# The front of a hybrid block rewritten in another order: angles, row statistics, squares and low products

## The chip, the cores and the metric

The kernel runs on one core of a Trainium2 chip. The metric is the device time of one execution in microseconds (us); the profile's own times are in us too, unless marked ns. TensorE is called PE here, its weight loads PEld, VectorE DVE, ScalarE ACT, GpSimd POOL, and SyncE, which issues most of the transfers, SP. L171 is line 171 of the kernel.

## The reference

The block is one layer of a decoder with a final norm: 1024 positions of width 1024. The input is normalised, modulated by a vector that comes from a condition `c`, and multiplied by one wide matrix whose columns feed attention with a window, a gated recurrent branch, and gates.

```python
mod = c @ w_ada[l] + b_ada[l]
shift, scale, gate = jnp.split(mod, 3, axis=-1)
h = rmsnorm(x, norm_g[l]) * (1.0 + scale[:, None, :]) + shift[:, None, :]
proj = h @ w_in[l]
q, k, v, g_attn, xr, g_rnn, m_attn, m_rnn = jnp.split(proj, SPLIT_POINTS, axis=-1)
...
merged = (jax.nn.sigmoid(m_attn) * (y_attn @ w_attn_proj[l])
          + jax.nn.sigmoid(m_rnn) * (y_rnn @ w_rnn_proj[l]))
x = x + gate[:, None, :] * (merged @ w_out[l])
return rmsnorm(x, final_g)
```

`q` and `k` are turned by angles that come from the positions (`partial_rope`). Here only the way to `h`, the first columns of `proj` and the angles matter.

## The kernel before, in words

The order of instructions is written by hand: each engine runs what the program lists for it, in that order, and waits for others by semaphores. The change touches the **front**, from the start of the program to the first products of V.

**Layout.** `h` is kept transposed: 128 input channels on the partitions, the 1024 positions along the free axis, so there are eight channel blocks, `kc` = 0 to 7, called channels below. Every block exists in two halves of 512 positions (`hf` = 0, 1). To multiply with nearly f32 precision, each operand is split in a rounded high part and the remaining low part: `hh` and `hl` for `h`, `wh` and `wl` for the weights. A product is three matmuls of 512 columns: `wh` by `hh` and `wl` by `hh` (terms "h"), and `wh` by `hl` (terms "l"). `hha`, `hhb`, `hla`, `hlb` in the profile are the halves for the channels 0 to 3, `hh` and `hl` both halves for 4 to 7.

**What the front computes.** Four column blocks of `proj` (`starts`), each with two accumulators of 512 positions in PSUM (`pmain` twice, and the banks `bk`), over the eight channels: 4 x 8 x 2 x 3 = 192 matmuls.

**What feeds them.** For channel `kc`:
- `modulate(kc, a)` (L241, DVE) multiplies a block of `w_ada` (`wada`, from `w_ss` in DRAM) with `c` spread over all partitions (`c_bc`) and sums it: a = 0 gives the shift, a = 1 the scale, and after it `gsc` (L245).
- `norm(kc)` (L371, DVE) multiplies the transposed input `xT` with `r_bc`, the root of each position's mean square, spread over the partitions. For channel 0 it reads the bank directly, one half at a time (L368).
- `affine(kc)` (L378, ACT) applies scale and shift in place; `high` (L374) or a cast (L478, ACT) makes `hh`; `low(kc)` (L383, DVE) makes `hl` by subtraction.

**The row statistics.** `x` also comes in eight tiles of 128 positions (`xt`). `square(i)` (L254, ACT) sums the squares of one. When four are done, `mean` (L352, DVE), `root_of` (L357, ACT) and the reciprocal in `spread` (L361, DVE) follow, and four transposes on PE (L363) spread the result over the partitions of a bank. Each half of the positions has its own such step.

**Weights.** `cast_w(i, h)` (L102 or L104, ACT) and `rest_w(i, h)` (L108 or L110, DVE) split half `h` (four channels) of the weights of block `i`. V's weights are split by the same two lines.

**Angles.** `angles()` reduces position times frequency to a turn in 29 small steps on DVE (128 x 64 mostly); the calls of `some(n)` take the next n of its pieces. `table()` takes the sine on ACT (L342) and writes a table to DRAM through POOL's queue.

**Fillers.** Four f32 matmuls of `ident` with `xt` (L421) and one with `r_bc` (L430) write a bank that nobody reads.

**Transfers.** All input loads of the front go through SP's queue in the order written. `wada` and `xt` share seven buffers, the halves of weights (`r`) six; a load into a buffer in use waits on SP, and the ones behind it wait too.

Of the kernel before, what the change touches and what calls it, by code (L numbers as in the profile page):

```python
# [12 lines left out]
F32 = mybir.dt.float32  # L13
# [9 lines left out]
P = 128  # L23
S = 1024
D = 1024
# [13 lines left out]
PAD_S = 544  # L39
# [13 lines left out]
def tile_hybrid_block(ctx, tc, x, x_t, pk, rows, posr, posi, c_row, w_ss, w_gate, w_main, w_v,  # L53
# [4 lines left out]
    def dma(dst, src, eng=nc.sync):  # L58
        dst, src = (a.bitcast(F32) if a.dtype == F32R else a for a in (dst, src))
        return eng.dma_start(dst, src)  # L60
# [126 lines left out]
    with ExitStack() as st:  # L187
# [10 lines left out]
        root = sp.tile([P, 1], F32, name="root")  # L198
        rr = sp.tile([P, 8], F32, name="rr")
# [7 lines left out]

        def load_ss(kc):
            for a in range(2):
                wa_t = sp.tile([P, D + 1], F32, tag="wada", name="wada", bufs=7)  # L210
                dma(wa_t[:], w_ss[a * D + kc * P:a * D + (kc + 1) * P, :])
                wada[kc, a] = wa_t
# [4 lines left out]
        def load_xt(kc):  # L217
            dma(xT[kc][:], x_t[kc * P:(kc + 1) * P, :])
# [6 lines left out]
        load_ss(0)  # L225
        for i in range(4):
            load_x0(i)
        load_xt(0)
        load_wh(0, 0)
# [5 lines left out]
        V.memset(c_bc[:, D:], 1.0)  # L235
        for hf in range(2):
            T.matmul(bk[2 + hf], one[0:1, :], c_row_t[:, SL[hf]], start=True, stop=True)

# [13 lines left out]
        def square(i):  # L252
            junk = sp.tile([P, D], BF16, tag="junk", name="junk")
            A.activation(junk[:], xt[i], AF.Square, accum_out=rr[:, i:i + 1])  # L254

# [94 lines left out]
        def mean(hf):  # L350
            r1 = rr[:, 4 * hf:4 * hf + 4]
            V.tensor_scalar(out=r1, in0=r1, scalar1=1.0 / D, scalar2=EPS, op0=ALU.mult,  # L352
                            op1=ALU.add)

        def root_of(hf):
            r1 = rr[:, 4 * hf:4 * hf + 4]
            A.activation(r1, r1, AF.Sqrt)  # L357
# [47 lines left out]
        some(7)  # L405
        V.tensor_copy(c_bc[:, SL[0]], bk[2])
        some(2)
        V.tensor_copy(c_bc[:, SL[1]], bk[3])
        for a in range(2):
            modulate(0, a)  # L410
        square(0)
        load_x0(5)
        load_x0(6)
        square(1)
        load_x0(7)
        for i in range(1, 4):
            load_wh(i, 0)
        square(2)
# [3 lines left out]
        load_ss(1)  # L422
        load_xt(1)
        mean(0)
        root_of(0)
        some(2)
        spread(0)
        some(2)
        A.copy(r_bc[:, SL[0]], bk[0])
# [4 lines left out]
        load_ss(2)  # L434
        load_xt(2)
        for i in range(2):
            load_wh(i, 1)
        rest_w(0, 0)
        high(0, 0)
# [12 lines left out]
        cast_w(2, 0)  # L452
        high(0, 1)
        affine(0, SL[1])
        rest_w(2, 0)
        A.copy(r_bc[:, SL[1]], bk[1])
        cast_w(3, 0)
        low(0, (1,))
        for a in range(2):
            modulate(1, a)  # L460
            if not a:
                rest_w(3, 0)
        for hf in range(2):
            for i in range(4):
                w, ps = starts[i]
                for ww, xx_ in ((w[0][0], hh), (w[0][1], hh), (w[0][0], hl)):
                    T.matmul(ps[hf], ww[:, 0:P], xx_[0][hf], start=(ww is w[0][0] and xx_ is hh),
                             stop=False)
        load_ss(3)
        load_xt(3)  # L470
# [3 lines left out]
        for kc in range(1, KC):  # L474
            norm(kc)
            affine(kc)
            for hf in range(2):
                A.copy(hh[kc][hf], xT[kc][:, SL[hf]])  # L478
# [10 lines left out]
            if kc + 3 < KC:  # L489
                load_ss(kc + 3)  # L490
                load_xt(kc + 3)
            if kc == 3:
                rv = [load_half(w_v[i // 2][:, SL[i % 2]]) for i in range(4)]
            if kc < 3:
                for terms in ("h", "l"):
                    for w, ps in starts:
                        mm_k(ps, w, kc, terms=terms)
            else:
                for i in (2, 3, 0, 1):
                    w, ps = starts[i]  # L500
# [1325 lines left out]
```

## Time and profile before

| | us |
|---|---|
| Three runs | 933.85, 934.57, 935.89 (median 934.57) |
| The profiled execution's own time | 935.91 |
| Its span in the trace | 934.2 |
| PE busy in the span | 909.0 |
| DVE busy | 680.8 |
| ACT busy | 533.8 |
| First product of the front | 24.39 |
| First product of V, behind the front | 76.85 |

The span is the time from the first to the last instruction of the trace; what lies around it is in the execution's own time. In rows of the timeline the first column is the start in us, the second the duration, then engine, line, operation, what it writes and reads, and the shape; in brackets stands how long the engine was idle just before, and what ended that. Matmuls overlap: of two in a row the second starts before the first has ended, so the distance of their starts is their price. The granted clock is the share of its full clock that PE was given.

### The profile page before, as it was taken

Reading aid. Unit: us, or ns where it says so; the run is one execution under the profiler, and the core shown is the slowest. Engines: PE = TensorE matmul, PEld = TensorE weight load, DVE = VectorE, ACT = ScalarE, POOL = GpSimd, SP = SyncE. Lnnn points to the kernel's source line nnn. Section 1 sums busy time; section 2 is a strip of 40 time slices with the busy share of each in tenths; the row PEclk is TensorE's granted clock in tenths of the full one; section 3 lists DMA queues with packets and bytes.
Section 4 is the critical chain, followed back from the end, with each engine's and each line's share of the span. In section 5 each row is a group of like instructions: output and inputs, shape, how many; then the busy total and the mean of one; then the engine's idle time right before and its main releaser. Section 6 shows DMA issues by size and latency. Waiting matters only on the chain.

```text
span 934.2 us, 12299 instructions
## 1 busy us (share of the span) xinstructions
PE 909.0 (97%) x4227; PEld 749.4 (80%) x4227; DVE 680.8 (73%) x1041; ACT 533.8 (57%) x1028; POOL 86.6 (9%) x146
## 2 busy tenths in 40 slices
PE   5999999999999999999999999999999999999997
PEld 1679888887888888888887888788888888888886
DVE  5895879887768973987688575799999737657422
ACT  5552566554557755875687785788888622213211
POOL 0120000000000000000000001354454300000000
PEclk9899999999999999999999999999999999999998
DMA  9942457864323351354245258997656186536311
GB/s 353 414 180 92 145 193 252 282 235 145 113 80 124 135 192 34 122 161 169 72 142 191 73 185 270 328 330 218 225 178 191 57 313 223 163 121 239 135 72 63
DMA packets 82147, 168.39 MB, mean 180 GB/s; under 512 B 12755, under 2 KB 29139, under 8 KB 82086
## 3 DMA queue, kind: packets, MB, share of 16 engines
q1 hardware_dynamic: 78596, 159.47, 50.0%
q0 software_dynamic: 2192, 6.00, 1.9%
q10 hardware_dynamic: 1298, 2.15, 0.6%
q8 instruction: 33, 0.54, 0.2%
q14 instruction: 28, 0.23, 0.1%
HBM read 118.20 MB, written 49.78 MB: 180 GB/s over the span
## 4 chain that ended last, share of the span: by engine, by line
PE 78%; DVE 9%; DMA 8%; ACT 2%; issue 2%; POOL 0%; SPq 0%; ACTq 0%; DVEq 0%
PE bk L648 43%; PE rp L171 8%; PE pgate L942 5%; PE rp L1689 4%; PE bk L171 4%; PE pmain L1689 4%; PE s_ps L1192 2%; PE pv L1264 2%; DMA smr<-smr_d 2%; PE pmain L171 1%; DMA wo<-w_out 1%; DMA tt<-tr_d 1%; PE pt L1230 1%; DVE wl L108 1%; DMA r<-w_ap 1%
## 5 line engine op out<-in xcount | busy, mean ns | idle before, releaser
L648 PE MATMUL bk<-nh,wl 128*128 128x512 f32 x352 | 137.3, 390 | 0.4 <-DVE wl L108 0.4
L648 PE MATMUL bk<-nh,wh 128*128 128x512 f32 x352 | 137.1, 389 | 0.0
L648 PE MATMUL bk<-nl,wh 128*128 128x512 f32 x352 | 137.0, 389 | 0.0
L108 DVE TENSOR_TENSOR wl<-r,wh 128x512 fp32r<-128x512 f32 x109 | 78.9, 729 | 23.3 <-ACT wh L102 23.3
L102 ACT CAST wh<-r 128x512 fp32r<-128x512 f32 x109 | 66.9, 618 | 42.3 <-PE bk L1437 13.2
L648 PEld LDWEIGHTS bk<-nh,wl 128*128 128x128 f32 x352 | 66.1, 188 | 15.0 <-DVE wl L108 1.4
L648 PEld LDWEIGHTS bk<-nh,wh 128*128 128x128 f32 x352 | 66.1, 188 | 13.7
L648 PEld LDWEIGHTS bk<-nl,wh 128*128 128x128 f32 x352 | 66.1, 188 | 13.6
L648 PE MATMUL bk<-hh,wh 128*128 128x512 f32 x176 | 68.6, 390 | 0.0
L648 PE MATMUL bk<-hh,wl 128*128 128x512 f32 x176 | 68.5, 389 | 0.0
L648 PE MATMUL bk<-hl,wh 128*128 128x512 f32 x176 | 68.5, 389 | 0.0
L108 DVE TENSOR_TENSOR wl<-ws,wh 128x512 fp32r<-128x512 f32 x76 | 51.5, 683 | 0.5 <-ACT wh L102 0.5
L1216 ACT ACTIVATE p<-p,small 128x129 f32<-128x129 f32 x128 | 50.1, 401 | 0.0
L102 ACT CAST wh<-ws 128x512 fp32r<-128x512 f32 x76 | 45.8, 614 | 3.3 <-DMA hla<-yl_d 1.6
L60 POOL DMA_DIRECT2D yh_d<-yh x1 | 0.6, 555 | 494.6 <-ACT yh L1009 494.6
L1706 ACT ACTIVATE o<-xo 128x1024 f32<-128x1024 f32 (+2 forms) x10 | 8.9, 889 | 53.2 <-DVE xo L1705 53.2
L648 PEld LDWEIGHTS bk<-hh,wh 128*128 128x128 f32 x176 | 33.0, 188 | 7.7 <-ACT wh L102 0.9
L648 PEld LDWEIGHTS bk<-hl,wh 128*128 128x128 f32 x176 | 33.0, 188 | 6.9
L648 PEld LDWEIGHTS bk<-hh,wl 128*128 128x128 f32 x176 | 33.0, 188 | 6.8
L1192 PE MATMUL s_ps<-ks,qs 128*128 128x256 f32 (+1 forms) x256 | 37.6, 289 | 0.1
L751 ACT ACTIVATE c<-bk 128x512 f32<-128x512 f32 x29 | 17.3, 597 | 30.3 <-PE bk L648 30.2
L648 PE MATMUL bk<-hha,wl 128*128 128x512 f32 x88 | 34.4, 390 | 0.1
(383 smaller groups left out, 2287.0 us busy)
## 6 DMA issues: line engine op xcount, KB each, us to landing
r<-w_main SPq DMA_DIRECT2D x100, 256.0 KB, 4.2
wada<-w_ss SPq DMA_DIRECT2D x16, 512.5 KB, 8.2
qs<-q_d SPq DMA_DIRECT2D x16, 512.0 KB, 5.9
ks<-k_d SPq DMA_DIRECT2D x24, 192.0 KB, 3.9
xT<-x_t SPq DMA_DIRECT2D x8, 512.0 KB, 8.8
q_d<-rhi SPq DMA_DIRECT2D x16, 256.0 KB, 4.1
q_d<-rlo SPq DMA_DIRECT2D x16, 256.0 KB, 3.7
sma_d<-c SPq DMA_DIRECT2D x16, 256.0 KB, 2.5
```

The costliest lines, as they stand in the source:

```text
L102: A.copy(dst[0][:], src)
L108: V.tensor_tensor(out=dst[1][:], in0=src, in1=f32(dst[0][:]), op=ALU.subtract)
L171: mm = T.matmul(ps[hf], ww, xx[kc][hf], start=(kc == 0 and ww is w_h and xx is xh), stop=(kc == KC - 1 and xx is xl))
L648: W["pe"] = T.matmul(ps, ww[:, c], b[kc][xx_], start=(first and kc == 0 and i == 0), stop=(kc == 3 and i == 2), skip_group_check=not first)
L751: A.activation(t["t"], s(), AF.Tanh, scale=0.5)
L942: W["pe"] = T.matmul(ps[:, SL[hf]], ww[:, c0:c0 + P], xx_[:, SL[hf]], start=(ic == 0 and i == 0), stop=(ic == 1 and i == 2))
L1192: W["pe"] = T.matmul(o, qs[:, j, qc], ks[:, b, k0 + (0 if n else P):k0 + 256], start=(b == 0), stop=(b == 1))
L1216: A.activation(px[:, j, :], px[:, j, :], AF.Exp, bias=sm[:, 0, j:j + 1], accum_out=sm[:, 1, j:j + 1])
L1230: W["pe"] = T.transpose(pt[:, j, :], px[:, j, 0:P], ident[:])
L1264: W["pe"] = T.matmul(pv[:], b, m[:].rearrange("p j q -> p (j q)"), start=(i == 0), stop=(i == len(prods) - 1))
L1689: T.matmul(ps[:, sl], lhs[k][th][:, ts_], w[:, sl], start=(k == 0 and w is h_ and lhs is mh), stop=(k == KC - 1 and lhs is ml))
L1706: A.activation(o[:, sl], xo[:, sl], AF.Square, accum_out=fs[:, i:i + 1])
```

## The change

It rewrites the front; the mathematics stays. In the order of the program:

- **Angles** (`some`): 22 of the steps stand ahead of modulate(0, 0), the other seven behind it. Before they were dealt out over the first 23 us.
- `c_bc` is copied out of the bank by ACT instead of DVE. The two `wada` of channel 0 are loaded apart, the second behind `xT` of channel 0.
- **Squares**: 5 and 7 go to DVE (`square_v`), the others stay on ACT. `mean` goes, and its factor and epsilon become scale and bias of the root.
- **Fillers** go.
- `spread(1)` follows `root_of(1)` at once, so that its transposes stand on PE behind the first two products; both copies of `r_bc` follow it on ACT.
- **norm** is called one channel ahead: norm(kc + 1) stands in the pass of `kc`, ahead of modulate(kc + 1). For channel 1 `high` makes `hh` straight from `xT`, before `affine`.
- **Low products one channel behind**: PE takes the "h" terms of `kc`, then the "l" terms of `kc` - 1.
- `xT` and `wada` are loaded a channel sooner, `xT` first; the second halves of the weights later; V's weights last. V's rests all stand behind the loop. `table()` moves from channel 1 to 2.

```diff
-        load_ss(0)
+        load_a(0, 0)
         for i in range(4):
             load_x0(i)
         load_xt(0)
+        load_a(0, 1)
         load_wh(0, 0)
         load_x0(4)
...
+            A.copy(c_bc[:, SL[hf]], bk[2 + hf])
...
+        def square_v(i):
+            jk = sp.tile([P, D + 1], BF16, tag="junk2", name="jk")
+            V.scalar_tensor_tensor(out=jk[:, :D], in0=xt[i], scalar=1.0, in1=xt[i],
+                                   op0=ALU.mult, op1=ALU.mult, accum_out=rr[:, i:i + 1])
...
-            A.activation(r1, r1, AF.Sqrt)
+            A.activation(r1, r1, AF.Sqrt, scale=1.0 / D, bias=eps[:])
...
+        some(16)
         square(0)
-        load_x0(5)
-        load_x0(6)
+        modulate(0, 0)
+        for i in (5, 6, 7):
+            load_x0(i)
+        for i in range(1, 4):
+            load_wh(i, 0)
         square(1)
-        load_x0(7)
-        for i in range(1, 4):
-            load_wh(i, 0)
         square(2)
+        some(99)
+        load_xt(1)
+        load_ss(1)
         square(3)
-        for i in range(4):
-            T.matmul(bk[1], ident[:], xt[i][:, :HALF], start=True, stop=True)
...
+        modulate(0, 1)
+        load_xt(2)
+        load_ss(2)
         root_of(0)
-        some(2)
         spread(0)
-        some(2)
-        A.copy(r_bc[:, SL[0]], bk[0])
-        T.matmul(bk[1], ident[:], r_bc[:, SL[0]], start=True, stop=True)
         cast_w(0, 0)
         norm(0, 0)
+        high(0, 0)
+        rest_w(0, 0)
+        terms_of(0, 0, (0,), "h")
         square(4)
+        square_v(5)
         affine(0, SL[0])
-        square(5)
         low(0, (0,))
-        some(99)
         square(6)
-        square(7)
-        mean(1)
+        square_v(7)
         root_of(1)
+        spread(1)
         cast_w(1, 0)
-        spread(1)
+        A.copy(r_bc[:, SL[0]], bk[0])
         rest_w(1, 0)
+        A.copy(r_bc[:, SL[1]], bk[1])
         norm(0, 1)
...
         for kc in range(1, KC):
-            norm(kc)
-            affine(kc)
-            for hf in range(2):
-                A.copy(hh[kc][hf], xT[kc][:, SL[hf]])
             if kc == 1:
+                for hf in range(2):
+                    high(kc, hf)
+                affine(kc)
+            else:
+                affine(kc)
+                for hf in range(2):
+                    A.copy(hh[kc][hf], xT[kc][:, SL[hf]])
+            if kc == 2:
                 table()
             if kc + 1 < KC:
+                norm(kc + 1)
                 for a in range(2):
                     modulate(kc + 1, a)
...
+            if kc == 1:
+                for hf in range(2):
+                    terms_of(kc, hf, range(4), "h")
+            elif kc < KC - 1:
+                for w, ps in starts:
+                    mm_k(ps, w, kc, terms="h")
+                for w, ps in starts:
+                    mm_k(ps, w, kc - 1, terms="l")
             else:
-                for i in (2, 3, 0, 1):
-                    w, ps = starts[i]
-                    mm_k(ps, w, kc)
+                last = [starts[i] for i in (2, 3, 0, 1)]
+                for w, ps in last:
+                    mm_k(ps, w, kc, terms="h")
+                for w, ps in last:
+                    for k in (kc - 1, kc):
+                        mm_k(ps, w, k, terms="l")
             if kc in (5, 6, 7):
                 for i in ((0,), (1,), (2, 3))[kc - 5]:
-                    wv.append(split(slot(), rv[i]))
+                    wv.append(slot())
+                    cast(wv[i], rv[i])
+        for i in range(4):
+            rest(wv[i], rv[i])
```

Three places of the new order matter below. The first is DVE's queue between the first scale and the first low part of channel 0, before (`rr` are the sums of squares, `sb`, `tt` and the like steps of the angles, `wl` a rest of weights):

```order
L241 SCALAR_TENSOR_TENSOR jk_276,mods_216<-wada_226,c_bc_212 128x1025
L245 SCALAR_TENSOR_TENSOR gsc_217<-mods_216,pk_t_75 128x1
L352 TENSOR_SCALAR rr_219<-rr_219 128x4
L270 TENSOR_SCALAR ra_309<-sa_269 128x64
L276 TENSOR_TENSOR fa_311<-sa_269,ra_309 128x64
L361 RECIPROCAL rr_219<-rr_219 128x4
L299 TENSOR_SCALAR sb_318<-t2_256 128x64
L302 SCALAR_TENSOR_TENSOR sb_318<-t1_260,sb_318 128x64
L302 SCALAR_TENSOR_TENSOR sb_318<-t0_264,sb_318 128x64
L315 TENSOR_TENSOR tt_322<-fa_311,sb_318 128x64
L368 TENSOR_TENSOR xT_190<-xT_190,bk0_68 128x512
L108 TENSOR_TENSOR wl_327<-r_237,wh_326 128x512
```

The same place of the changed kernel, down to norm(0, 1) and one rest behind it:

```order
L248 SCALAR_TENSOR_TENSOR jk_328,mods_216<-wada_236,c_bc_212 128x1025
L252 SCALAR_TENSOR_TENSOR gsc_217<-mods_216,pk_t_75 128x1
L368 RECIPROCAL rr_220<-rr_220 128x4
L375 TENSOR_TENSOR xT_190<-xT_190,bk0_68 128x512
L108 TENSOR_TENSOR wl_343<-r_238,wh_342 128x512
L265 SCALAR_TENSOR_TENSOR jk_352,rr_220<-xt_298 128x1024
L390 TENSOR_TENSOR hla0_160<-xT_190,hha0_158 128x512
L265 SCALAR_TENSOR_TENSOR jk_358,rr_220<-xt_301 128x1024
L368 RECIPROCAL rr_220<-rr_220 128x4
L108 TENSOR_TENSOR wl_372<-r_303,wh_371 128x512
L375 TENSOR_TENSOR xT_190<-xT_190,bk1_69 128x512
L110 SCALAR_TENSOR_TENSOR wl_379<-r_305,wh_378 128x512
```

The angles and the mean are gone from here, two squares (L265) stand between, and modulate(0, 1) with its scale is the row right ahead of the first reciprocal.

The second place is DVE's queue in the pass of channel 3, before (`xT3_193` is channel 3, `xT_194` channel 4):

```order
L371 TENSOR_TENSOR xT3_193<-xT3_193,r_bc_188 128x1024
L241 SCALAR_TENSOR_TENSOR jk_523,mods_216<-wada_446,c_bc_212 128x1025
L241 SCALAR_TENSOR_TENSOR jk_525,mods_216<-wada_448,c_bc_212 128x1025
L245 SCALAR_TENSOR_TENSOR gsc_217<-mods_216,pk_t_75 128x1
L110 SCALAR_TENSOR_TENSOR wl02_208<-r_425,wh02_207 128x512
L110 SCALAR_TENSOR_TENSOR wl03_210<-r_427,wh03_209 128x512
L383 TENSOR_TENSOR hla3_172<-xT3_193,hha3_170 128x512
L383 TENSOR_TENSOR hlb3_173<-xT3_193,hhb3_171 128x512
```

And in the changed kernel:

```order
L378 TENSOR_TENSOR xT_194<-xT_194,r_bc_188 128x1024
L248 SCALAR_TENSOR_TENSOR jk_516,mods_216<-wada_422,c_bc_212 128x1025
L248 SCALAR_TENSOR_TENSOR jk_518,mods_216<-wada_424,c_bc_212 128x1025
L252 SCALAR_TENSOR_TENSOR gsc_217<-mods_216,pk_t_75 128x1
L110 SCALAR_TENSOR_TENSOR wl02_208<-r_426,wh02_207 128x512
L110 SCALAR_TENSOR_TENSOR wl03_210<-r_428,wh03_209 128x512
L390 TENSOR_TENSOR hla3_172<-xT3_193,hha3_170 128x512
L390 TENSOR_TENSOR hlb3_173<-xT3_193,hhb3_171 128x512
```

Only the first row differs: it is norm of channel 4 where it was norm of channel 3.

The third place is PE's queue at the first products of channel 3 with the banks 2 and 3, before:

```order
L171 MATMUL bk2_70<-hha3_170,wh_379 128x512
L171 MATMUL bk3_71<-hhb3_171,wh_379 128x512
L171 MATMUL bk2_70<-hha3_170,wl_380 128x512
L171 MATMUL bk3_71<-hhb3_171,wl_380 128x512
L171 MATMUL bk2_70<-hla3_172,wh_379 128x512
L171 MATMUL bk3_71<-hlb3_173,wh_379 128x512
```

In the changed kernel, from the last "h" terms of channel 3 on:

```order
L171 MATMUL bk0_68<-hha3_170,wl_385 128x512
L171 MATMUL bk1_69<-hhb3_171,wl_385 128x512
L171 MATMUL pmain_254<-hla2_168,wh_342 128x512
L171 MATMUL pmain_254<-hlb2_169,wh_342 128x512
L171 MATMUL pmain_255<-hla2_168,wh_371 128x512
L171 MATMUL pmain_255<-hlb2_169,wh_371 128x512
```

Before, `hla3` is read by the fifth product of the channel; now all sixteen "h" terms of channel 3 and the eight "l" terms of channel 2 run first, and `hla3` is read after the "h" terms of channel 4.

More of the change, by code (lines that the diff above doesn't have):

```diff
@@ L453, in tile_hybrid_block @@
         high(0, 1)
+        rest_w(2, 0)
         affine(0, SL[1])
-        rest_w(2, 0)
-        A.copy(r_bc[:, SL[1]], bk[1])
         cast_w(3, 0)
+        norm(1)
+        modulate(1, 0)
+        rest_w(3, 0)
         low(0, (1,))
[L459 to L462, printed above, removed]
-        for hf in range(2):
-            for i in range(4):
-                w, ps = starts[i]
[L466 to L470, printed above, removed]
+        modulate(1, 1)
+        terms_of(0, 0, (0,), "l")
+        for i in (1, 2, 3):
+            for terms in "hl":
+                terms_of(0, 0, (i,), terms)
+        terms_of(0, 1, range(4), "h")
+        terms_of(0, 1, range(4), "l")
+        for i in range(2):
+            load_wh(i, 1)
+        load_xt(4)
+        load_ss(4)
         for i in (2, 3):
```

56 lines of the change are left out of this document (23 added, 33 removed).

## The prediction

> **What bounds the kernel now.** I read the busy shares first, then the busy time by stretch, then TensorE (PE) and VectorE (DVE) in order of time.
>
> ```profile
> PE 909.0 (97%) x4227; PEld 749.4 (80%) x4227; DVE 680.8 (73%) x1041; ACT 533.8 (57%) x1028; POOL 86.6 (9%) x146
> ...
> 24.30:76.90 52.60, 49.04 (x196) 38.21 (x195) 44.34 (x73) 28.60 (x42) 8.41 (x13) 0.93 0.68 264
> 76.90:130.00 53.10, 53.00 (x324) 47.50 (x323) 38.56 (x54) 26.37 (x41) 0.00 (x0) 1.00 0.44 153
> 130.00:934.20 804.20, 794.33 (x3691) 658.58 (x3689) 585.11 (x870) 464.37 (x920) 77.45 (x127) 1.00 0.51 171
> ```
>
> In the stretches the columns are length, busy time of PE, its weight loads, DVE, ScalarE (ACT) and GpSimd, then granted clock, DMA share and GB/s. After 76.9 us PE is busy almost all the time, so the program is bound by TensorE's own products there. The change touches only what lies ahead. There 192 products of 512 columns must run, and they take from 24.39 to 76.85.
>
> ```profile
> 24.39 0.78 PE L467 MATMUL pmain<-hha,wh 128*128 128x512 f32 x1
> ...
> 48.69 0.75 PE L171 MATMUL bk<-hla,wh 128*128 128x512 f32 x1 [1.50 <-DVE hla L383]
> ...
> 52.33 0.39 PE L171 MATMUL pmain<-hha,wh 128*128 128x512 f32 x1
> ...
> 76.85 0.28 PE L1435 MATMUL bk<-wh,hha 128*128 128x256 f32 x1
> ```
>
> The first row is the first product, the last the first one of V's projection, behind the front. Of the 192, 72 belong to channels 0 to 2 and 12 of channel 3 start before 52.33, so 108 run from there: 24.52 / 108 = 0.227 us each, without a pause. All 192 at that pace are 43.6 us of the 52.46. The last wait ends at 48.69: PE stands for `hla` of channel 3, and nothing ahead of that sets the end. So the front ends at that moment plus 116 products, 8 of them at half rate.
>
> ```profile
> 21.40:24.80 3.40, 1.17 (x5) 1.18 (x6) 2.41 (x11) 2.69 (x7) 0.00 (x0) 0.51 1.02 417
> 24.80:28.20 3.40, 3.40 (x9) 2.38 (x8) 2.27 (x4) 2.63 (x4) 0.00 (x0) 0.50 1.02 412
> ...
> 45.30:48.70 3.40, 1.77 (x7) 0.68 (x5) 2.96 (x7) 1.93 (x4) 0.00 (x0) 1.00 1.05 402
> 48.70:52.10 3.40, 3.40 (x8) 2.46 (x9) 3.37 (x5) 1.66 (x2) 0.00 (x0) 0.51 1.04 419
> ```
>
> Those 8 ran under half the clock: 8 products in 3.4 us where 15 fit, so that one such stretch costs 7 x 0.227 = 1.6 us. It follows a stretch in which PE had 1.77 us of work.
>
> **What one channel costs on VectorE.** PE waited for DVE, so the price list is DVE's. These rows are the pass of channel 1: norm(1), modulate(2) twice with its read of the sum, the scale of channel 2, low(1) twice, norm(2).
>
> ```profile
> 30.91 1.22 DVE L371 TENSOR_TENSOR xT<-xT,r_bc 128x1024 f32<-128x1024 f32 x1
> 32.04 1.22 DVE L241 SCALAR_TENSOR_TENSOR jk<-wada,c_bc 128x1025 bf16<-128x1025 f32 x1
> ...
> 33.30 1.23 DVE L241 SCALAR_TENSOR_TENSOR jk<-wada,c_bc 128x1025 bf16<-128x1025 f32 x1
> ...
> 34.58 0.16 DVE L245 SCALAR_TENSOR_TENSOR gsc<-mods,pk_t 128x1 f32<-128x1 f32 x1
> 34.65 0.69 DVE L383 TENSOR_TENSOR hla<-xT,hha 128x512 fp32r<-128x512 f32 x1
> ...
> 35.85 1.22 DVE L371 TENSOR_TENSOR xT<-xT,r_bc 128x1024 f32<-128x1024 f32 x1
> ...
> 40.09 1.29 DVE L108 TENSOR_TENSOR wl<-r,wh 128x512 fp32r<-128x512 f32 x2 [0.36 <-ACT wh L102]
> ...
> 42.51 1.22 DVE L371 TENSOR_TENSOR xT<-xT,r_bc 128x1024 f32<-128x1024 f32 x1
> ```
>
> Start to start: norm 1.13, modulate 1.27, scale 0.08, each half of low 0.60, a pass 4.94. Channel 2 adds two rests of weights (0.60 each) and a wait of 0.36 and some tenths: 6.66. The same steps stand in the new order at the same prices. What differs is the lead: before, norm(k) follows low(k-1), and ACT's affine and cast follow norm(k); after, norm(k) has been done a pass earlier and ACT starts as soon as the scale of k is there. The high part of a channel comes 1.20 + 1.13 = 2.3 us sooner for that alone. Second, PE takes the low products one channel late, so that the wait of 48.69 (low(3), behind modulate(4) and two rests) can't recur.
>
> **The new path, step by step.** The second half of the rows' statistics decides when that list may begin. The first two rows give the time from issue to landing, the others the issues.
>
> ```profile
> xT<-x_t SPq DMA_DIRECT2D x1, 512.0 KB, 8.7
> ...
> xt<-x SPq DMA_DIRECT2D x1, 512.0 KB, 9.7
> ...
> 4.83 0.44 SPq L60 DMA_DIRECT2D xT<-x_t  x1
> ...
> 9.84 0.33 SPq L60 DMA_DIRECT2D xt<-x  x1
> ```
>
> The second `wada` is issued five places later, right behind xT of channel 0, so it lands when that one did: 4.83 + 8.7 = 13.5. This is an added wait: modulate(0,1) now stands on DVE ahead of the first reciprocal, and behind it queue the reciprocal, norm(0,0) and the first rest, for which ACT's `hha` and PE's first product wait.
>
> ```profile
> 15.14 0.60 PE L363 MATMUL bk<-ident,rr 128*128 128x128 f32 x4
> 23.63 1.11 PE L363 MATMUL bk<-ident,rr 128*128 128x128 f32 x4 [6.09 <-DVE rr L361]
> ...
> 15.77 0.58 ACT L429 COPY r_bc<-bk 128x512 f32<-128x512 f32 x1 [1.77 <-PE bk L363]
> 16.77 1.06 ACT L254 ACTIVATE junk<-xt 128x1024 bf16<-128x1024 f32 x1
> 17.82 0.80 ACT L374 ACTIVATE hha<-xT,mods,gsc 128x512 fp32r<-128x512 f32 x1
> 18.66 0.81 ACT L378 ACTIVATE xT<-xT,mods,gsc 128x512 f32<-128x512 f32 x1
> ...
> 16.39 0.69 DVE L368 TENSOR_TENSOR xT<-xT,bk 128x512 f32<-128x512 f32 x1 [1.32 <-ACT r_bc L429]
> 19.51 0.69 DVE L383 TENSOR_TENSOR hla<-xT,hha 128x512 fp32r<-128x512 f32 x1 [1.83 <-ACT xT L378]
> ...
> 23.39 0.18 DVE L361 RECIPROCAL rr<-rr 128x4 f32<-128x4 f32 x1 [0.27 <-ACT rr L357]
> 24.78 0.69 DVE L368 TENSOR_TENSOR xT<-xT,bk 128x512 f32<-128x512 f32 x1 [0.19 <-PE bk L363]
> 25.50 0.82 ACT L374 ACTIVATE hhb<-xT,mods,gsc 128x512 fp32r<-128x512 f32 x1 [1.10 <-DVE xT L368]
> ```
>
> 13.5 + 1.27 + 0.1: reciprocal at 14.9. From reciprocal to norm I take 1.39 (23.39 to 24.78): the transposes then took 1.11 at half clock, 0.60 at full clock behind the fillers that go, so the second price is the one left. Norm(0,0) at 16.3, against 16.39. `hha` 0.72 later at 17.0, square 4 at 17.85, affine 1.05 later at 18.9, low(0,0) 0.85 later at 19.75, square_v(7) at 20.35; its rows of x have landed at 9.84 + 9.7 = 19.5. Its price isn't shown. Modulate, one element wider and with the same read of a sum, has 1.27; a pass without that read (norm) 1.13; I take 1.27, the nearer form, so 21.6. Root and reciprocal as before, 0.3: 21.9 instead of 23.39. Transposes until 23.3; norm(0,1) now waits also for ACT's copy out of the same bank, 0.62 (15.77 to 16.39): 23.9 instead of 24.78.
>
> From 23.9 DVE has norm half and rest (1.20), norm(1) 1.13, modulate 1.15, rest and low half 1.20, modulate and scale 1.35: norm(2) at 29.9 (before 35.85). Then one pass of 4.94 and two of 6.15 with their rests: norm(5) at 47.2. The two waits of 0.4 before rests need not recur, since ACT's casts no longer wait behind norm; the sine table now stands ahead of the first of them on ACT, so I keep both waits as a bound, 0.8. Norm(5), modulate(5) and scale end 3.75 later, at 50.9. ACT's affine and casts then cost what these rows of channel 4 show:
>
> ```profile
> 50.41 1.24 ACT L378 ACTIVATE xT<-xT,mods,gsc 128x1024 f32<-128x1024 f32 x1 [3.18 <-DVE xT L371]
> 51.68 1.15 ACT L478 CAST hh<-xT 128x512 fp32r<-128x512 f32 x2
> ```
>
> 1.27 to the cast, some 0.6 for its first half and as much for the second: `hh` of channel 5 at 52.9 and 53.4. By then PE has taken 112 products. At the last weights of channel 0, 28.1, it has 10 behind it, and 28.1 + 102 x 0.227 = 51.3; by the same steps it stands 0.7 and 0.5 for the halves of channel 2 and 0.3 for channel 4, which makes 52.8, so both arrive together. 80 products are left, with one pause of 0.5 for the second half: 52.9 + 0.5 + 80 x 0.227 = 71.6; without the pause 71.1; with the waits 72.4. That is 4.4 to 5.8 before 76.85; I take **5.0**, near the middle.
>
> Costs put at nothing, and their cover. The 29 small angle steps, some 0.22 each (below), are 6.4 us between 2.6 and 13.5, where DVE has only a modulate beside them. `c_bc`'s two copies go to ACT, which waits for x there; epsilon costs one memset. The five f32 products that go stood in PE's waits. SP's queue brings each xT ahead of its two `wada` and a channel sooner; at 412 GB/s one takes 1.27, and the tightest, `wada`(1,0), lands near 24 (13.5 and six such transfers and four half ones) where DVE asks at 26.2. V's four rests come after low(7), at 67, and PE wants them at 71.6; without that cover each costs 0.60. V's products also need two banks that ACT copies (about 0.6 each, as at 15.77): 12 products, 2.7 us, lie between.
>
> ```profile
> 13.89 0.22 DVE L276 TENSOR_TENSOR fa<-sa,ra 128x64 f32<-128x64 f32 x1
> ```
>
> Does the rest follow? ACT's row says so.
>
> ```profile
> 95.76 0.62 ACT L102 CAST wh<-r 128x512 fp32r<-128x512 f32 x1 [13.21 <-PE bk L1437]
> ```
>
> ACT stood 13 us for PE there, with DVE behind it, so both have room ahead of it and restart from PE's own progress. I carry the 5.0 over in full: the profiled execution's own 935.91 (span 934.2 and 1.7 around it) becomes 930.9. It lies 1.3 above the median of the three runs, so the forecast is 934.57 - 5.0 = **929.6**.
>
> **A rule weighed.** A half-rate stretch followed one with 1.77 us of work and no idle piece over 1.5. The Trainium skill, "TensorE: Matmul & The Clock Gate", section "Part 1: The HAM clock gate", says that the clock halves after a whole idle window of about 3.4 us and returns after a busy one; the trace agrees on the length, 48.70 to 52.10, but not on the wholly idle window. By the rule alone, the new front would have half the clock only at its start, and the sum stays.
>
> **The rivals.** (1) *A pause lowers the clock again.* Half-rate once more among the last 80 products: 1.6 us, so 931.2. Against it: the pauses I find there are half a microsecond, in stretches 80% busy. (2) *The first spread hangs on a late transfer.* Everything on the path is behind `wada`(0,1). Each microsecond that it lands after 13.5 is lost one for one; 3.5 late gives 933.1, no change. For it: the copy sits in a stream at 400 GB/s. Against: that landing is read off the same place in the stream. (3) *PE never warms.* Without fillers, and with waits for weights between 22 and 31, the clock stays at half. PE has 182 products left at 28.1, 41.3 us at full rate, 69.4; each at half rate costs 0.2 more. From 37 such products, 16 us of half clock, the front ends after 76.85; six such stretches, until 48.6, are 48 such products: 79.0, and 936.7, slower. Against it: from 28.1 PE has work without a pause over 1, and in the stretch 24.80 to 28.20 such work brought the clock back.
>
> **How the numbers follow.** Forecast 0.74 (928.8 to 930.2 by its bounds, and a microsecond on each side for the runs' spread of 2.0), rival 1 0.13, rival 2 0.08, rival 3 0.05. The range 927.8 to 932.2 takes the first two with that microsecond. About 0.2%, 1.9 us, is what a measurement tells from no change: faster 0.87, the same 0.08, slower 0.05.
>
> **What would show it.** V's first product at 71 to 73; norm(2) on DVE near 29.9 and norm(5) near 47.2; first reciprocal near 14.9 and the second near 21.9; no wait of PE for `hla` or `hlb` past channel 0, and granted clock 1.00 from 32 on. The forecast is wrong if PE still waits over a microsecond after 45, or if DVE's norm(2) comes after 32.

## The result, and the profile after

| | kernel before | changed kernel |
|---|---|---|
| median (runs) | 935.89 (7) | 931.44 (7) |
| lowest, highest | 933.85, 937.38 | 929.74, 932.77 |
| ratio, 95% interval | | 0.9954, 0.9940 to 0.9967 |
| profiled execution, its span | 935.91, 934.2 | 932.08, 929.9 |
| first product / first of V's projection | 24.39 / 76.85 | 17.81 / 71.50 |

The change makes the kernel faster by 0.46% (0.33 to 0.60), 4.3 us of 935.9. The first view is the busy time by stretch of the changed kernel, cut where V's projection begins; columns as in the prediction.

```profile
17.80:71.50 53.70, 48.68 (x196) 37.41 (x197) 46.20 (x77) 32.77 (x50) 6.90 (x13) 1.00 0.78 305
71.50:130.00 58.50, 58.41 (x348) 52.01 (x347) 41.67 (x60) 30.04 (x48) 0.00 (x0) 1.00 0.47 165
130.00:929.90 799.90, 789.15 (x3668) 654.21 (x3666) 582.93 (x867) 461.40 (x915) 77.91 (x127) 1.00 0.51 171
```

The front ends 5.35 us earlier; behind it PE is as full as it was. DVE's timeline of the changed kernel has the steps that the prediction gave times for: modulate(0,1), the two reciprocals, norm(0,1), norm(2), norm(5).

```profile
13.43 1.23 DVE L248 SCALAR_TENSOR_TENSOR jk<-wada,c_bc 128x1025 bf16<-128x1025 f32 x1 [2.93 <-DMA wada<-w_ss]
...
14.78 0.17 DVE L368 RECIPROCAL rr<-rr 128x4 f32<-128x4 f32 x1
...
21.80 0.18 DVE L368 RECIPROCAL rr<-rr 128x4 f32<-128x4 f32 x1 [0.42 <-ACT rr L364]
...
23.80 0.69 DVE L375 TENSOR_TENSOR xT<-xT,bk 128x512 f32<-128x512 f32 x1 [0.80 <-ACT r_bc L458]
...
29.84 1.22 DVE L378 TENSOR_TENSOR xT<-xT,r_bc 128x1024 f32<-128x1024 f32 x1
...
47.12 1.22 DVE L378 TENSOR_TENSOR xT<-xT,r_bc 128x1024 f32<-128x1024 f32 x1
```

Predicted were 13.5, 14.9, 21.9, 23.9, 29.9 and 47.2. PE's timeline has its two last waits in the front, and V's first product.

```profile
35.65 0.51 PE L171 MATMUL pmain<-hha,wh 128*128 128x512 f32 x1 [0.53 <-ACT hha L491]
...
52.41 0.39 PE L171 MATMUL bk<-hlb,wh 128*128 128x512 f32 x1
52.94 1.02 PE L171 MATMUL pmain<-hh,wh 128*128 128x512 f32 x2
...
71.50 0.28 PE L1459 MATMUL bk<-wh,hha 128*128 128x256 f32 x1
```

Predicted was 71.6. The second wait is short and stands in two parts: the product at 52.94 starts 0.53 behind the one ahead of it instead of 0.227, and its second half waits some 0.4 more, so that the two last 1.02 where 0.62 is usual. No wait for a low part is left behind channel 0. But the span is only 4.3 shorter, not 5.35. Set side by side, the two programs run with a shift of 5.35 to 5.4 from V's first product until the scores of the attention stage (`s_ps`, near 582 in the kernel before); 1.6 of it is lost at one product there and 0.3 right behind, and 0.5 comes back near 860. In the three fences: PE and ACT of the changed kernel, then ACT of the kernel before at the same instruction.

```profile
579.18 0.98 PE L1216 MATMUL s_ps<-ks,qs 128*128 128x256 f32 x6 [1.37 <-DVE p L1230]
```

```profile
577.26 0.62 ACT L102 CAST wh<-ws 128x512 fp32r<-128x512 f32 x1 [3.68 <-DMA hla<-yl_d]
577.78 0.58 ACT L1224 COPY p<-s_ps 128x512 f32<-128x512 f32 x1
```

```profile
580.61 0.62 ACT L102 CAST wh<-ws 128x512 fp32r<-128x512 f32 x1 [1.65 <-DMA hla<-yl_d]
```

ACT stood 3.68 behind a transfer instead of 1.65, DVE behind ACT's copy of the scores, PE behind DVE. Whether the change causes this, or one execution's transfers, a single profile can't tell; nor whether the half-rate stretch of 48.70 in the kernel before, priced at 1.6 us by the prediction, belongs to it.

### The profile page after: what moved, and what is told of

Read it like the earlier page. It is cut to its first block, busy times and chain, and to the rows that moved or that the text cites. A ratio compares the mean times of both kernels' runs of the same rounds, so it can differ in the third digit from the quotient of the medians.

```text
span 929.9 us, 12279 instructions
## 1 busy us (share of the span) xinstructions
PE 901.1 (97%) x4217; PEld 745.5 (80%) x4217; DVE 681.1 (73%) x1042; ACT 533.2 (57%) x1026; POOL 85.5 (9%) x146
## 4 chain that ended last, share of the span: by engine, by line
PE 87%; DVE 7%; DMA 3%; issue 1%; ACT 1%; SPq 0%; POOL 0%; ACTq 0%; DVEq 0%
PE bk L672 43%; PE rp L171 12%; PE pmain L171 6%; PE rp L1713 5%; PE pgate L966 5%; PE pmain L1713 4%; PE bk L171 3%; PE s_ps L1216 2%; PE pv L1288 2%; DVE jk L248 1%; PE pt L1254 1%; DMA wada<-w_ss 1%; DMA ks<-k_d 1%; PE bk L1461 1%; PE bk L1460 1%
## 5 line engine op out<-in xcount | busy, mean ns | idle before, releaser
L102 ACT CAST wh<-r 128x512 fp32r<-128x512 f32 x109 | 66.9, 618 | 43.4 <-PE bk L1461 11.6
L672 PEld LDWEIGHTS bk<-nh,wl 128*128 128x128 f32 x352 | 66.1, 188 | 15.1 <-DVE wl L108 1.4
L775 ACT ACTIVATE c<-bk 128x512 f32<-128x512 f32 x29 | 17.3, 598 | 29.9 <-PE bk L672 29.9
```

Source lines behind the costliest of these rows:

```text
L102: A.copy(dst[0][:], src)
L672: W["pe"] = T.matmul(ps, ww[:, c], b[kc][xx_], start=(first and kc == 0 and i == 0), stop=(kc == 3 and i == 2), skip_group_check=not first)
L775: A.activation(t["t"], s(), AF.Tanh, scale=0.5)
```

## The experiments

The measure is the start of V's first product in each profile ("V"), with the ratio of times to the kernel before, in the same group of runs, beside it. Each edit is to the kernel named.

**The kernel before, once more** (no edit), and **the changed kernel, once more** (no edit).

> The kernel before, once more. In its first profile there was half the clock from 48.77 to 52.18, and no wait of PE for DVE near 583, where the changed kernel waits 1.4. Theory A (both are chance of an execution: the start of the clock's stretches against the program, and one slow transfer): a half-rate stretch at another place or none behind 30, and a wait near 583 of up to 1.8. Theory B (both belong to the order of the work): the stretch within 48 to 53 again, and no wait near 583.

> The changed kernel, once more. Theory A (where a half-rate stretch falls is chance of an execution): V's first product at 71.5, or at 72.5 to 72.9 with half the clock somewhere between 26 and 32, as the kernel with low products in step had it there with the same program up to 31; the wait near 579 anywhere from 0.2 to 1.8; the whole 3.3 to 5.4 us below the kernel before. Theory B (the new order keeps the clock up by itself, and the wait of 1.4 is the price of its earlier front): 71.5 and full clock from 26 on, and 1.4 near 579 again.

PE's timeline of the kernel before, second execution, its second reciprocal on DVE, and its busy time in the two stretches around the wait:

```profile
47.95 0.50 PE L171 MATMUL bk<-hla,wh 128*128 128x512 f32 x1 [1.49 <-DVE hla L383]
...
74.77 0.28 PE L1435 MATMUL bk<-wh,hha 128*128 128x256 f32 x1
```

```profile
22.66 0.18 DVE L361 RECIPROCAL rr<-rr 128x4 f32<-128x4 f32 x1 [0.27 <-ACT rr L357]
```

```profile
44.20:47.61 3.41, 2.11 (x7) 0.86 (x5) 2.97 (x6) 2.25 (x5) 0.00 (x0) 1.00 1.04 406
47.61:51.02 3.41, 2.97 (x12) 2.23 (x13) 3.37 (x6) 1.32 (x2) 0.00 (x0) 1.00 1.04 415
```

The same wait, 1.49 against 1.50, and no half rate behind it. The clock is decided in stretches of 3.41 us, and here their borders cut the wait so that the fuller part has 2.11 of PE's work, where 1.77 stood in the first profile. V comes at 74.77 instead of 76.85, 2.08 earlier: 0.73 because the first product was that much earlier, and 1.35 for the half-rate stretch. (At full rate the eight products behind the wait would save 1.6, but PE then stands a few tenths for `hlb`, so the stretch costs less than the prediction's price.) The wait of PE for DVE near 581 is 0.5. Of the 0.73, 0.3 is the landing of x, by which the fillers begin, and 0.4 the clock's doing. PE's timeline, first the first profile, then the second, with the four f32 products of x by the identity (the fillers, eight records) and the transposes of the first spread:

```profile
8.66 6.64 PE L421 MATMUL bk<-xt,ident 128*128 128x512 f32 x8 [2.35 <-DMA xt<-x]
15.14 0.60 PE L363 MATMUL bk<-ident,rr 128*128 128x128 f32 x4
```

```profile
8.34 6.23 PE L421 MATMUL bk<-xt,ident 128*128 128x512 f32 x8 [2.19 <-DMA xt<-x]
14.40 0.60 PE L363 MATMUL bk<-ident,rr 128*128 128x128 f32 x4
```

DVE's reciprocals, at 14.03 and 13.74, were ready before; the transposes wait in PE's queue for the end of the fillers, which took 6.64 and 6.23 by when the clock rose (14.6 and 13.5). In a third execution of the same beginning (the kernel with the order of products alone, below) it rose at 11.6, the fillers took 5.32 and the transposes came at 13.89, right behind the reciprocal of 13.65.

The changed kernel's second execution, two rows of PE's timeline and the stretch around the first of them:

```profile
28.47 0.63 PE L419 MATMUL bk<-hla,wh 128*128 128x512 f32 x1
28.90 0.63 PE L419 MATMUL pmain<-hhb,wh 128*128 128x512 f32 x1
...
71.40 0.28 PE L1459 MATMUL bk<-wh,hha 128*128 128x256 f32 x1
```

```profile
27.20:30.60 3.40, 2.92 (x7) 2.16 (x7) 3.37 (x8) 0.80 (x2) 0.00 (x0) 1.00 1.03 416
```

PE ran at half rate until 30.6 (0.43 from one product to the next), and V still came at 71.40. The 1.0 to 1.4 that theory A put down for that are missing, since PE's wait at 35 was gone instead. The wait near 579 was 0.2. Median of ten runs 930.21, ratio 0.9956 (0.9939 to 0.9972). So theory A holds for both in this: where a stretch falls, and the later wait, are chance.

How often a stretch falls is another matter, and the record of the unprofiled runs shows it. One stretch at half rate lowers an execution's mean granted clock by 0.0018 (half of 3.41 in 934); it is 0.992 in the first profile of the kernel before and 0.994 in the second. Of the 74 executions of that kernel in the groups of runs below, 35 have 0.992 or less, so at least one stretch more than the second profile, somewhere in the program; 27 have 0.994 or more. Their mean times are 935.8 and 934.1. About half the executions of the kernel before pay for such a stretch: chance picks the execution, but the first profile is no rare one.

The span behind V was 858.4 and 856.6 in the two profiles of the changed kernel, 857.4 and 857.8 in those of the kernel before: no price of the change shows there. The two profiles of each put V at 75.8 and 71.45 in the mean, 4.4 apart; the times show 4.3.

**The lead taken back** in the changed kernel.

```diff
         for kc in range(1, KC):
+            if kc > 1:
+                norm(kc)
...
             if kc + 1 < KC:
-                norm(kc + 1)
                 for a in range(2):
```

> The changed kernel, but from channel 2 on norm(k) stands again at the head of channel k's own pass, behind low(k-1). Measure: the start of V's first product (76.85 before, 71.50 in the changed kernel). Theory A (the prediction's step: the lead is worth the 1.20 + 1.13 = 2.3 us that stand between): 73.8. Theory B (without the lead DVE also stands in low(k) for ACT's affine, since affine and casts start only behind norm and take 2.4 us while DVE has 2.5 us of modulate, and a wait of that kind comes back in each pass with a cast of weights): over 75, up to 75.9, nearly the whole gain gone. Theory C (the lead doesn't matter, PE's own products are the bound): under 72.

V at 75.98; 935.48 against 935.30, ratio 1.0003 (0.9990 to 1.0016). Theory B: the gain is gone. DVE's timeline of this kernel shows that the lead covers more than the 2.3 between its two places:

```profile
39.73 1.29 DVE L108 TENSOR_TENSOR wl<-r,wh 128x512 fp32r<-128x512 f32 x2 [2.00 <-ACT wh L102]
...
46.37 1.29 DVE L110 SCALAR_TENSOR_TENSOR wl<-r,wh 128x512 fp32r<-128x512 f32 x2 [0.40 <-ACT wh L104]
```

The casts of weights stand on ACT behind affine, casts and the sine table of channel 2 (1.28 to load it, 0.31 to use it); with norm late all of that starts late, and DVE, which has its modulates done, stands 2.00 for them there and 0.40 in channel 3. The waits that the prediction kept as a bound of 0.8 are absent in the changed kernel only because of the lead: 2.3 + 2.4 = 4.7, of which 4.5 show (75.98 - 71.45). The lead alone is not worth all of that: in the kernel before, whose sine table stands in channel 1, the first of the two waits is 0.36, so some 1.6 of the 4.5 (an estimate, 2.00 - 0.36) is the table's new place, which only the lead covers. No run moves the table alone.

**Low products in step** in the changed kernel: each channel's low products right behind its own high ones.

```diff
                 for hf in range(2):
                     terms_of(kc, hf, range(4), "h")
+                for w, ps in starts:
+                    mm_k(ps, w, kc, terms="l")
             elif kc < KC - 1:
-                for w, ps in starts:
-                    mm_k(ps, w, kc, terms="h")
-                for w, ps in starts:
-                    mm_k(ps, w, kc - 1, terms="l")
+                for terms in "hl":
+                    for w, ps in starts:
+                        mm_k(ps, w, kc, terms=terms)
...
```

(The first hunk is channel 1, whose low products now follow at once; channel 7 is changed in the same way.)

> The changed kernel, but each channel's low products stand right behind its own high products of all four accumulators (channels 1 to 7), not one channel behind. Theory A (the prediction's second reason, the lag is what keeps PE from waiting for the low parts): PE waits over 1 us for hla or hlb again, near 46, perhaps with a half-rate stretch behind, and V's first product is at 72.5 to 74.6. Theory B (sixteen high products are cover enough, and low products of channel 1 fill the wait of 0.7 before channel 2 at 34.7 instead): waits of a few tenths at 40.5 and 46.5, V's first product at 70.7, 0.8 earlier than in the changed kernel.

PE's busy time in two stretches of this profile:

```profile
25.11:28.52 3.41, 1.76 (x6) 0.82 (x6) 3.41 (x6) 1.68 (x3) 0.00 (x0) 1.00 1.03 416
28.52:31.93 3.41, 3.41 (x10) 2.64 (x9) 3.37 (x6) 1.82 (x3) 0.00 (x0) 0.50 1.02 410
```

V at 71.11 (theory B 70.7), and no wait of PE for a low part; the 0.7 before channel 2 is filled as well. That in spite of a stretch of half clock at 28.5 (the second row). 929.55, ratio 0.9941 (0.9920 to 0.9962). Theory A is refuted: the lag is not what keeps PE from waiting.

**The order of products alone**, and **the lead alone**, in the kernel before.

```diff
-            if kc < 3:
-                for terms in ("h", "l"):
-                    for w, ps in starts:
-                        mm_k(ps, w, kc, terms=terms)
-            else:
-                for i in (2, 3, 0, 1):
+            for terms in ("h", "l"):
+                for i in (0, 1, 2, 3) if kc < 3 else (2, 3, 0, 1):
                     w, ps = starts[i]
-                    mm_k(ps, w, kc)
+                    mm_k(ps, w, kc, terms=terms)
```

> The kernel before, but in channels 3 to 7 PE takes the high products of all four accumulators and then the low ones, where it took both of one accumulator before the next. Nothing else differs. Theory A (lead or lag are needed): PE still waits over 1 us near 48 and V's first product is at 76 to 77. Theory B (the wait of 48.69 is one of order alone): no wait for hla at 48.69, granted clock 1.00 from 48.7 to 52.1, V's first product at 74.6: 0.7 of the wait and 1.6 of half clock gone, with a wait of some 0.9 for hh of channel 4 near 52.

```diff
         for kc in range(1, KC):
-            norm(kc)
+            if kc == 1:
+                norm(kc)
...
             if kc + 1 < KC:
+                norm(kc + 1)
                 for a in range(2):
```

> The kernel before, with only norm(k+1) moved ahead of modulate(k+1), from channel 2 on; PE's order is that of before. Theory A (the lead is worth 2.3 us in itself): V's first product at 74.5. Theory B (the lead brings the high parts earlier but puts one norm, 1.13, ahead of low(3), for which PE stood at 48.69): PE waits 2.5 to 3.1 us there, half the clock behind it, and V's first product is at 76.5 to 77.4, no gain.

Order alone: no wait for `hla` at 48.7, a short one for `hh` as foretold; V at 73.35, though this profile has a half-rate stretch at 28.7; it is 1.2 below theory B's 74.6 because the second reciprocal came at 22.21 here and at 23.39 in the profile from which that was reckoned; 933.87 against 935.30, ratio 0.9981 (0.9967 to 0.9995). PE's timeline:

```profile
51.16 1.02 PE L171 MATMUL bk<-hh,wh 128*128 128x512 f32 x2 [0.62 <-ACT hh L478]
```

Lead alone: PE waits longer for the low part, as theory B said:

```profile
48.07 0.49 PE L171 MATMUL bk<-hla,wh 128*128 128x512 f32 x1 [2.40 <-DVE hla L383]
...
74.89 0.28 PE L1437 MATMUL bk<-wh,hha 128*128 128x256 f32 x1
```

V lies below theory B's 76.5 because no half rate followed in this execution; beside the 74.77 of the kernel before without such a stretch the lead gains nothing. 936.63 against 935.30, ratio 1.0011 (0.9997 to 1.0025): no change.

**Both together** in the kernel before.

> The kernel before with the two edits that were run apart: norm(k+1) ahead of modulate(k+1) from channel 2 on, and in channels 3 to 7 the high products of all four accumulators ahead of the low ones. Apart, the order of products moved the whole by -1.8 us and the lead by +1.0 (no change). Theory A (they need each other: the lead brings high parts sooner and low parts later, and only an order that takes high parts first can use that): V's first product at 72.0 to 73.2, by whether the first product is at 23.2 or 24.4, and the whole 2.5 to 3.5 us below the kernel before. Theory B (each is worth what it was apart): 73.4 to 74.9, and -1.8 or less.

DVE's second reciprocal and V:

```profile
22.32 0.18 DVE L361 RECIPROCAL rr<-rr 128x4 f32<-128x4 f32 x1 [0.27 <-ACT rr L357]
```

```profile
71.94 0.28 PE L1433 MATMUL bk<-wh,hha 128*128 128x256 f32 x1
```

931.46 against 935.87, ratio 0.9959 (0.9942 to 0.9975). Theory A, and 4.4 in the times where 2.5 to 3.5 were expected: two edits, -0.2% and no change apart, bring -0.4% together, about as much as the whole rewritten front. The start of the second reciprocal on DVE, from which the chain of channels runs, tells what each part of the change is worth (runs of the next paragraphs included):

| profile | second reciprocal | V | from one to the other |
|---|---|---|---|
| kernel before, first and second | 23.39, 22.66 | 76.85, 74.77 | 53.46, 52.11 |
| with the order alone | 22.21 | 73.35 | 51.14 |
| with the lead alone | 22.58 | 74.89 | 52.31 |
| with both | 22.32 | 71.94 | 49.62 |
| changed kernel, first and second | 21.80, 21.64 | 71.50, 71.40 | 49.70, 49.76 |
| its lead taken back | 21.70 | 75.98 | 54.28 |
| its squares on ACT | 23.18 | 72.88 | 49.70 |
| its second `wada` early | 20.84 | 70.55 | 49.71 |

Behind the second reciprocal the lead and the order together do all that the rewritten front does: 49.6 against 49.7. The rest of the change only moves that reciprocal, by 0.4 to 1.6 against the five profiles that begin as the kernel before does. The first product, 5.5 earlier in the changed kernel than here (17.81 against 23.32), brings nothing by itself.

**Squares 5 and 7 on ACT**, and **the second `wada` early**, in the changed kernel.

```diff
-        square_v(5)
+        square(5)
...
-        square_v(7)
+        square(7)
```

> The changed kernel, with the squares 5 and 7 back on ACT, as before the change. Theory A (the second spread stands on the path, so what delays its reciprocal delays all behind it): ACT has four squares and an affine behind hha at 16.95, the second reciprocal comes 1.4 to 1.7 later, at 23.2 to 23.5 instead of 21.80, and V's first product at 72.9 to 73.2. Theory B (PE's waits behind it, 0.7 near 35 and 0.7 near 53, and DVE's 2.5 us freed take it up): V's first product at 71.5 to 71.9.

```diff
-        load_a(0, 0)
+        load_ss(0)
...
-        load_a(0, 1)
```

> The changed kernel, with the second wada tile issued right behind the first, as before the change, so that it lands some 6 us earlier and the four first x tiles 1.3 later. Theory A (the first spread hangs on that transfer, microsecond for microsecond, and all behind it follows): first reciprocal 13.6 instead of 14.78, second 20.6, V's first product 70.3. Theory B (behind it the landing of the last x tile, 19.6, is what decides): first reciprocal 13.6, second 21.1 to 21.8, V's first product 70.9 to 71.5. Theory C (x lands later and the first spread gains nothing): 14.8 and 71.5.

The two reciprocals on DVE, first with the squares on ACT, then with the early transfer:

```profile
14.69 0.17 DVE L368 RECIPROCAL rr<-rr 128x4 f32<-128x4 f32 x1
...
23.18 0.18 DVE L368 RECIPROCAL rr<-rr 128x4 f32<-128x4 f32 x1 [1.85 <-ACT rr L364]
```

```profile
13.62 0.18 DVE L367 RECIPROCAL rr<-rr 128x4 f32<-128x4 f32 x1 [1.85 <-ACT rr L363]
...
20.84 0.18 DVE L367 RECIPROCAL rr<-rr 128x4 f32<-128x4 f32 x1 [0.42 <-ACT rr L363]
```

Squares: the second reciprocal 1.38 later, V at 72.88, 1.38 later (932.76, ratio 0.9975, 0.9963 to 0.9987). Transfer: the first reciprocal 1.16 earlier, the second 0.96, V at 70.55, 0.95 earlier: between theories A and B. V follows the second reciprocal to a tenth. In the times the second shows nothing: 930.30, ratio 0.9956 (0.9941 to 0.9971).

**The fillers kept** in the changed kernel.

```diff
+        for i in range(4):
+            T.matmul(bk[1], ident[:], xt[i][:, :HALF], start=True, stop=True)
         modulate(0, 1)
```

> The changed kernel, with the four f32 products of x by the identity put back on PE ahead of the first spread (their sums are used by nothing). Theory A (the half clock ahead of 26 lies under waits for weights, so the fillers' removal cost nothing): first transposes 0.5 shorter, V's first product 71.3 to 71.8. Theory B (products ahead of 26 at half rate hold up the front, and the fillers would save it): 70.5 or less. Theory C (the fillers move the clock's stretches so that half clock falls on 20 to 27 and again behind): 72 to 73.

V at 70.77, between A and B: 0.5 of it is the transposes at full clock, the rest a first reciprocal at 14.52 instead of 14.78. The times show no difference (930.71, ratio 0.9955, 0.9939 to 0.9972).

**All together**: the changed kernel with the early `wada`, low products in step (their lines are left out here), and two reorderings; then with the fillers too.

```diff
-        load_a(0, 0)
+        load_ss(0)
...
-        load_a(0, 1)
...
-        for i in (1, 2, 3):
+        for terms in "hl":
+            terms_of(0, 0, (1,), terms)
+        terms_of(0, 1, (0, 1), "h")
+        for i in (2, 3):
             for terms in "hl":
                 terms_of(0, 0, (i,), terms)
-        terms_of(0, 1, range(4), "h")
+            terms_of(0, 1, (i,), "h")
         terms_of(0, 1, range(4), "l")
...
+            low(kc)
             if kc in (2, 3):
                 for i in (0, 1) if kc == 2 else (2, 3):
                     cast_w(i, 1)
                     rest_w(i, 1)
-            low(kc)
```

> The changed kernel with four edits: the second wada tile early; low products of each channel behind its own high ones, first half before second; channel 0's high products of the second half as soon as an accumulator's weights are there; low(2) and low(3) ahead of the casts of weights on DVE. Theory A (front bound by DVE's chain from the first spread on, PE's waits filled): V's first product at 68.8, or 70.2 with one stretch of half clock; the whole 2 to 3 us below the changed kernel, 928 to 930 beside 935 of the kernel before. Theory B (what the front gains is given back behind it): V's first product the same 68.8, but the whole no better than the changed kernel, 931 and more.

> The kernel with all four edits, and with the four f32 products of x by the identity in front of the first spread. Theory A (the shorter transposes are worth 0.5 to 0.7 here too): V's first product at 68.0 to 68.2, the whole 0.6 lower, 928.2, which the runs can hardly tell. Theory B (the clock falls to half behind the fillers and takes it back): 68.7 and more.

PE's waits from 26 to 70 us in the kernel with all four, with total, number and longest:

```profile
PE pmain L418 <- ACT hha L380: 0.7, 1, 0.7
PE pmain L426 <- DVE hl L389: 0.4, 1, 0.4
```

V at 68.68 (expected 68.8); 928.82 against 934.74, ratio 0.9932 (0.9919 to 0.9945): the best kernel here, 1.4 to 2.6 below the two medians of the changed one, which are of other groups of runs. With the fillers V was 69.44 and the time the same, 928.79 (ratio 0.9927, 0.9902 to 0.9951). They held PE until 15.1, and the transposes stood behind them though the reciprocal began at 13.85: theory B's outcome, by PE's queue. The clock has its part in it, since it rose only at 14.7 here and the fillers ran at half rate; with the fillers in the changed kernel, above, they began at 6.99 instead of 8.59, the clock rose at 11.75, and they ended before the reciprocal.

## Why the prediction was right, and where its reasons were not

- **DVE's chain** (the price list, norm(2) at 29.9, norm(5) at 47.2): right to about 0.1 us at every step, the second reciprocal and the 1.27 for `square_v` among them. The two experiments on the spreads show that this chain sets the end: V stands 49.7 behind the second reciprocal in both, as in the changed kernel.
- **V's first product** at 71.6: 71.50 and 71.40.
- **The sum, 5.0 of 935.91.** The term that was mis-sized is its base, V at 76.85 from a single execution. That profile held a half-rate stretch behind the wait of 48.69 (1.35 by the second profile, where the prediction has 1.6) and fillers that ended late; the second profile has 74.77. A front at 71.5 is then worth 3.3 to 5.35, 4.4 in the mean; measured were 4.3. The unprofiled runs agree: the means 935.8 and 934.1 lie 5.0 and 3.3 above 930.8, the mean of the 17 executions of the changed kernel (an estimate, since the groups of runs are not the same). So 5.0 is the gain over an execution with such a stretch, which about half of them have. Of the 1.8 by which the forecast of 929.6 lies below the measured 931.44, some 0.5 comes from there. The other 1.3 is the step down from the profiled execution's 935.91 to the median of three runs, 934.57: the median of seven is 935.89, so that the step was not needed.
- **"Second, PE takes the low products one channel late, so that the wait of 48.69 can't recur."** This reason failed. In step the wait doesn't recur either, and V comes no later. What removed it is that PE takes the sixteen high products of a channel before its low ones, which came with the same rewriting, together with the lead: the order alone takes the wait away (73.35), both bring V to 71.94.
- **"Comes 1.20 + 1.13 = 2.3 us sooner for that alone."** Too small for what hangs on it: 4.5 in this kernel, since two waits for casts come back without it, one of them grown by the sine table that the change moved. And nothing in the old order of products, where only the low part's lateness counts.
- **Rival 1** (half clock once more among the last 80 products): it did not come. What came in one profile is half rate until 30.6, where PE has waits that take it up (V at 71.40). Between 32 and the front's end neither profile of the changed kernel has any, as foretold; two profiles can't say how seldom it is.
- **Rival 2** (one for one with the second `wada`): the price was nearly right, 0.95 of 1.16, read the other way round; the landing was too: modulate(0,1), which waits for it, began at 13.43, against 13.5.
- **Rival 3** (PE never warms): PE stayed at half rate to 30.6 in one execution at no cost.
- **"I carry the 5.0 over in full."** Right on the mean of two profiles each: the stretch behind V is 857.4 and 857.8 before, 858.4 and 856.6 after.

## What to carry to other kernels

Moving one step ahead pays only if the order on the engine that uses it can take what comes early: here the lead alone brought no change and the order alone -0.2%, both together -0.4%. A single profile holds its own luck, here 2.1 us at the end of the front in the same kernel; before a stall or a half-rate stretch of it is counted as gain, look whether it stands in a second execution, and by the granted clock of the other runs how often it comes. To find what part of a rewritten stage matters, measure from the step on which the rest hangs: here the second reciprocal, and not the first product. And work put into an engine's idle time, like the fillers, is in the way as soon as it ends later than what stands behind it in the queue.

## What the hardware showed

- **The clock is decided by stretches of 3.41 us whose borders lie elsewhere in each execution.** In the fourteen traces it fell from full rate behind stretches with 1.76, 1.78, 1.86 and, in the kernel with the order of products alone at 588 to 592 us, 2.05 us of PE's work (busy time by modelled ends), and behind all with less than 1.4. It stayed up behind all with 2.07 or more, and behind ten with 1.62 to 1.97. So no sharp bound shows: stretches with 1.76 to 1.97 of 3.41 went both ways. From half rate it rose behind 2.80 to 2.98, not behind two with 3.0, so that there, too, no bound can be read. The Trainium skill, "TensorE: Matmul & The Clock Gate", section "Part 1: The HAM clock gate", says that the window runs freely, so that the place varies from run to run: these traces agree (the same wait of 1.5, with half rate behind it in one execution and without in the other). It also says that the rate falls after an idle window; here one that was about half full was often enough, so the measured stretches decide.
- **The granted clock of a profile begins with its first change.** The row of 27.20 in the changed kernel's second profile says 1.00 while products are 0.43 apart; from 31 on they are 0.227 apart. Ahead of the first change the rate is to be read from the spacing.
